# Three gate projections in the scans, 9,800 columns per scan step, preparation two gaps apart, and another order of scores and transposes in the attention

## The chip, the core and the metric

The kernel runs on one core of one Trainium2 chip. The core has five engines, each with its own instruction stream: TensorE (PE, matrix products; its weight loads, PEld, overlap them), VectorE (DVE), ScalarE (ACT), GpSimd (POOL) and SyncE (SP, which issues the DMAs of this kernel). Each of them executes its stream in order, and waits on semaphores for the others. The metric is the device time of one execution in microseconds (us); less is better. Every time given for a program is a median over several executions, and one further execution is recorded by the hardware profiler.

## The reference

One layer of a hybrid backbone: a gated DeltaNet of 8 heads and a grouped-query attention of 8 query heads read the same normalised input through one projection `w_in`; each head's output is multiplied by silu of a gate that is also a projection of that input; `w_out` closes the layer.

```python
def mixer(h, hc, w_in, conv_w, a_log, dt_bias, gdn_norm_w, q_norm_w, k_norm_w, w_out, cos, sin, with_ctx):
    qkv_g, z_g, gates, q_a, k_a, v_a, z_a = split_proj(h @ w_in)
    qkv_gc, z_gc, gates_c, q_ac, k_ac, v_ac, z_ac = split_proj(hc @ w_in)
    ql, kl, vl, bl, gl = gdn_inputs(qkv_g, gates, conv_w, a_log, dt_bias)
    qc, kc, vc, bc, gc = gdn_inputs(qkv_gc, gates_c, conv_w, a_log, dt_bias)
    ...
    o_lf, _ = chunk_gated_delta(ql, kl, vl, gl[0], bl[0], s_cf)
    ...
    gdn_lat = (rms_norm(o_gdn, gdn_norm_w).reshape(B, L, GDN_WIDTH) * jax.nn.silu(z_g))
    qa, ka, va = attn_heads(q_a, k_a, v_a, q_norm_w, k_norm_w)
    qa, ka = apply_rope(qa, cos, sin), apply_rope(ka, cos, sin)
    ...
    attn_lat = block_attention(qa, k_all, v_all) * jax.nn.silu(z_a)
    y = jnp.concatenate([gdn_lat, attn_lat], axis=-1) @ w_out
```

There are 512 latent tokens, 256 context tokens, a model width of 2048 and a head width of 128, all in float32. `z_g` and `z_a` are the gates: 8 heads of 128 columns each.

## The kernel before

Every matrix product of the projections is made of three, of a high and a low part of each operand (`whi`, `wlo`: ACT copies the high part of a weight piece, POOL subtracts to get the low one, both of 128x512). A projection of one head for the latent tokens is 16 blocks of rows x 3 = 48 matmuls of 512 columns; with the context tokens it has 48 of 256 columns more.

PE's order is the order in which the program is written (`manual_schedule` for PE), from the first scan to the end of the attention. DVE, ACT, POOL and SP are ordered by a scheduler in the first part, with raised priority for the recurrence; in the attention DVE, ACT and POOL stand in the written order as well. The stages, by the profile's time, are:

- *The start* (to 242 us): modulation, the projections of head 0, decay gates, preparation of head 0.
- *The scans* (242 to 922 us): `gdn_scan(h)` for 8 heads, one after the other. A head has 12 steps. A step is a recurrence between PE, DVE and ACT: `ks` (keys and queries on the state), `rh` on DVE, `ts` (solved block), `vs` and `vn` on ACT, the state's update `ts`, `st` on DVE, `o`. The generator yields up to three times in a step, with F1, F2, F3 = 3400, 2200, 2800; at each yield the loop *pulls* so many columns of other projections from `feeding()` (one matmul of 512 columns, or of 512 and 256, at a time). A yield is a gap, or slot; a head has 35 of them. Between heads the loop pulls on until the next head's k, q and v are made ("forced" pulls).
- *Preparation*: `gdn_prep(h + 1)` is a generator too, and its groups run in the slots of `PREP_AT` of head h: transposes of the keys t1, t2, t3 with their squares on ACT (`NT`, `ss`), Gram matrices `gq`, `gc`, the solve of small blocks (`NE` on DVE, through DRAM: `nd`, `NE`, `nd2`, `DD`), transposes of the values, then `DT` (a transpose of DD on DVE) and the products pxa, pxb, pxy in slots 27 to 33. t1 and t3 have one PSUM bank in turn, t2 and gq another. The end of a scan, its *tail* (squares, norm, scaling of `oq`, transposes `ot`), runs under the next head's slots.
- *Feeding*: q, k, v of head 1; three of the attention's keys and values (`kva`); k, q, v of the heads 2 to 7; the last `kva`; the eight attention queries `qa`, which go through DRAM (`qad`).
- *The attention* (922 to 1225 us): 17 units u, of which each has the scores of one head's half (`attn_scores`, softmax on DVE and ACT) and the transposes and values of the unit before (`attn_pt`, `attn_values`). `fill(n)` puts n times three matmuls of the gate projections between them: `fillers()` makes all 16 gates (64 pieces of 12 matmuls), and drives `gate_rows()`, which sums the rows of the residual's gate on ACT and POOL (`graw`, `gacc`). FS, FP, FQ, FR = 3, 3, 1, 3 are the numbers of fills behind the scores, behind each of three transposes, behind the values and at the unit's end. `z_over` turns a finished gate into silu and multiplies it with `M`, which holds the 16 heads' outputs.
- *The output projection* (from 1225 us).

In columns, the pulls ask for 110,500 ahead of the first scan, and for 12 x 8,400 - 3,400 = 97,400 in each scan. What there is to pull is 7 x 48 x 2048 (k, q, v) + 4 x 48 x 768 (kva) + 8 x 48 x 512 (qa) = 1,032,192.

## Time and profile before

| | |
|---|---|
| median of 3 runs | 1426.57 us (1420.46 to 1427.27) |
| the profiled execution | 1422.1 us |
| its span, first to last instruction | 1420.3 us |
| granted TensorE clock, mean | 0.982 |
| DMA | 161.95 MB, mean 114 GB/s |

In the rows of the profile that follow below, a line is "engine line operation output<-inputs"; buffer numbers are left out of the names, so `tsh` is the `ts` tile of any head and step, `rh` the `r` tile, `sth` the state. A row of waits has who waited for whom, the total in us, the number of waits and the longest. A row of the timeline begins with start and duration in us, and has the idle time ahead of it, with what ended it, in square brackets. Matmuls are pipelined: what one costs is the distance to the start of the next, not its duration.

### The profile page before, as it was taken

The numbers are of one execution on the slowest core, as the hardware profiler recorded it, in microseconds if no ns is written. First come the engines' busy times: TensorE is split into PE (matmuls) and PEld (weight loads), VectorE is DVE, ScalarE is ACT, GpSimd is POOL, SyncE is SP. The second block draws the span as 40 slices with busy tenths as digits, with TensorE's granted clock in tenths as the row PEclk, the third lists the DMA queues.
The fourth block names the chain that finished last, engine by engine and source line by source line (L and its number), as shares of the span: only waits on it lengthen the run. The fifth ranks groups of instructions, "written<-read, shape, count | busy, mean of one in ns | idle before, by whom it ended". The sixth has DMA issues, their size and how long they took to land. (4 is left out here: it accounts for less than half of the span.)

```text
span 1420.3 us, 24982 instructions
## 1 busy us (share of the span) xinstructions
PE 1282.4 (90%) x9406; PEld 1024.6 (72%) x9406; DVE 741.2 (52%) x1642; ACT 608.5 (43%) x1511; POOL 533.0 (38%) x477
## 2 busy tenths in 40 slices
PE   3888888999998989899898988989999999999997
PEld 1455677888777777777777767777777777777785
DVE  3444694533666766576756343155555555644322
ACT  4111343343545455544545444355555554433221
POOL 1011212334344343434343444466666665112320
PEclk9999999999999999999999999999999999999999
DMA  9999622322222213132222343454444442474202
GB/s 310 277 279 283 162 66 58 73 73 74 61 54 64 55 46 73 50 62 58 54 65 57 84 135 86 132 179 119 127 134 121 117 125 76 165 235 148 89 31 103
DMA packets 263323, 161.95 MB, mean 114 GB/s; under 512 B 62946, under 2 KB 236091, under 8 KB 262179
## 3 DMA queue, kind: packets, MB, share of 16 engines
q1 hardware_dynamic: 263203, 160.36, 41.0%
q8 instruction: 74, 1.21, 0.4%
q14 instruction: 46, 0.38, 0.1%
HBM read 147.54 MB, written 12.77 MB: 113 GB/s over the span
## 5 line engine op out<-in xcount | busy, mean ns | idle before, releaser
L122 POOL TENSOR_TENSOR wlo_z<-wraw_z,whi_z 128x512 fp32r<-128x512 f32 x64 | 92.5, 1448 | 80.4 <-ACT whi_z L121 72.1
L214 POOL TENSOR_TENSOR sdh<-sth,egl 128x256 f32<-128x256 f32 x80 | 55.7, 696 | 143.3 <-DVE sth L756 69.6
L1186 PE MATMUL zl<-hhL,whi_z 128*128 128x512 f32 x256 | 107.4, 420 | 0.0
L1186 PE MATMUL zl<-hlL,whi_z 128*128 128x512 f32 x256 | 101.6, 397 | 0.0
L1186 PE MATMUL zl<-hhL,wlo_z 128*128 128x512 f32 x256 | 101.3, 396 | 0.2 <-POOL wlo_z L122 0.2
L735 ACT ACTIVATE oqh<-ksh,egsw 64x128 f32<-64x128 f32 x128 | 46.6, 364 | 118.8 <-DVE rh L730 118.0
L730 DVE SCALAR_TENSOR_TENSOR rh<-ksh,negeg,vtokh 64x128 f32<-64x128 f32 x176 | 61.3, 348 | 53.7 <-PE ksh L718 41.5
L1225 POOL TENSOR_TENSOR gacc<-graw,gacc 128x512 f32<-128x512 f32 x60 | 85.1, 1418 | 0.5
L139 PE MATMUL po<-wlo_wo,mh 128*128 128x512 f32 x192 | 76.9, 401 | 1.8 <-DVE wlo_wo L122 1.8
L138 PE MATMUL po<-whi_wo,mh 128*128 128x512 f32 x192 | 77.0, 401 | 1.6 <-DVE M L214 1.1
L140 PE MATMUL po<-whi_wo,ml 128*128 128x512 f32 x192 | 76.7, 400 | 0.0
L756 DVE TENSOR_TENSOR sth<-sdh,tsh 128x256 f32<-128x256 f32 x80 | 33.7, 421 | 77.6 <-PE tsh L750 56.3
L122 DVE TENSOR_TENSOR wlo_wo<-wraw_wo,whi_wo 128x512 fp32r<-128x512 f32 x48 | 37.8, 794 | 59.5 <-ACT whi_wo L121 59.3
L1321 POOL TENSOR_TENSOR yx<-yx,tt 128x512 f32<-128x512 f32 x12 | 17.2, 1446 | 127.8 <-DVE tt L214 127.8
L750 PE MATMUL tsh<-vsh,ktok 128*128 128x128 f32 x352 | 59.2, 292 | 5.7 <-ACT vnh L746 5.7
L122 POOL TENSOR_TENSOR wlo_qa<-wraw_qa,whi_qa 128x512 fp32r<-128x512 f32 x32 | 41.4, 1295 | 53.0 <-ACT whi_qa L121 44.1
L743 ACT ACTIVATE vsh<-tsh,cch 128x128 f32<-128x128 f32 x88 | 32.3, 368 | 66.9 <-PE tsh L739 64.2
L750 PEld LDWEIGHTS tsh<-vsh,ktok 128*128 128x128 f32 x352 | 47.8, 195 | 18.0 <-ACT vnh L746 14.5
L815 DVE TENSOR_TENSOR ptl<-pt,pth 128x512 fp32r<-128x512 f32 x48 | 32.8, 683 | 53.5 <-ACT pth L814 53.5
L1103 DVE TENSOR_REDUCE mx<-s 128x1 f32<-128x768 f32 x32 | 30.5, 953 | 53.9 <-PE s L140 53.9
L1186 PEld LDWEIGHTS zl<-hhL,wlo_z 128*128 128x128 f32 x256 | 48.3, 189 | 12.4 <-POOL wlo_z L122 0.6
L1186 PEld LDWEIGHTS zl<-hhL,whi_z 128*128 128x128 f32 x256 | 48.5, 189 | 11.4 <-ACT whi_z L121 2.5
(398 smaller groups left out, 4045.7 us busy)
## 6 DMA issues: line engine op xcount, KB each, us to landing
wada<-in_w_ada SPq DMA_DIRECT2D x128, 256.0 KB, 5.2
wraw_z<-in_w_in SPq DMA_DIRECT2D x64, 256.0 KB, 2.9
graw<-in_w_ada SPq DMA_DIRECT2D x64, 256.0 KB, 3.0
wraw_wo<-in_w_out SPq DMA_DIRECT2D x48, 256.0 KB, 2.9
wraw_qa<-in_w_in SPq DMA_DIRECT2D x32, 256.0 KB, 2.8
wraw_q<-in_w_in SPq DMA_DIRECT2D x28, 256.0 KB, 2.9
wraw_k<-in_w_in SPq DMA_DIRECT2D x28, 256.0 KB, 2.9
wraw_v<-in_w_in SPq DMA_DIRECT2D x28, 256.0 KB, 2.9
```

Source lines behind the costliest of these rows:

```text
L122: (lo_eng or G).tensor_tensor(out=lo, in0=raw, in1=hi, op=ALU.subtract)
L138: T.matmul(out, lhsT=lh, rhs=rh, start=start, stop=False, skip_group_check=True)
L139: T.matmul(out, lhsT=lh, rhs=rl, start=False, stop=False, skip_group_check=True)
L140: T.matmul(out, lhsT=ll, rhs=rh, start=False, stop=stop, skip_group_check=True)
L214: eng.tensor_tensor(out=out, in0=x, in1=y, op=ALU.mult)
L730: V.scalar_tensor_tensor(out=r[rows], in0=ks[rows, d], scalar=gsc["negeg"][rows, gcol:gcol + 1], in1=vtok[rows, p], op0=ALU.mult, op1=ALU.add)
L735: S.activation(oq[rows, v, p - 2], ks[rows, d], AF.Copy, scale=gsc["egsw"][rows, gcol:gcol + 1])
L750: T.matmul(ts[:, d], lhsT=ktok[:, p, half], rhs=vs, start=True, stop=True, skip_group_check=True)
L756: V.tensor_tensor(out=sn, in0=sd, in1=ts[:, 0:2], op=ALU.add)
L815: V.tensor_tensor(out=lo, in0=ps_ap, in1=hi, op=ALU.subtract)
L1186: T.matmul(pl, lhsT=lw, rhs=rt[:, k], start=st, stop=sp, skip_group_check=True)
L1225: G.tensor_tensor(out=acc, in0=raw, in1=acc, op=ALU.add)
```

## The change

Four things are changed. (1) F1, F2, F3 become 3900, 2700, 3200: 9,800 columns per step, 113,700 per scan. The gates of three attention heads (`feed_za`, 3 x 48 x 512 columns) are added to the end of the feeding and go through DRAM (`zad`); there are then 1,105,920 columns to pull. `fillers()` leaves these three out, and units 0 to 2 of the attention take them from `M` (`zae`, `silu`); `attn_values` multiplies by half. (2) The groups of the preparation stand in slots 0, 2, 4, 6, 8, 10, 12 instead of 0, 1, 2, 3, 5, 7, 9; the last four stay. (3) The feeding puts one `kva` behind head 1 and each of the heads 2 and 3, and one `qa` behind each of the heads 4 to 7. (4) In a unit of the attention the first two transposes come ahead of the scores; FS, FV, FQ, FR = 4, 4, 1, 3 fills stand behind the scores, ahead of the values, behind them and at the end; the steps of the query's normalisation follow the scores. The rows of the residual's gate advance twice in four fills from the sixth piece on, instead of nine times in 32 fills from the start.

```diff
--- before.py
+++ after.py
@@ -17,8 +17,9 @@
 D = 2048
 KT = D // 128
 CA_BUFS = 1
-FS, FP, FQ, FR = 3, 3, 1, 3
+FS, FV, FQ, FR = 4, 4, 1, 3
 GB = 3
+NZA = 3
 SEQ = 512
 CTX = 256
 NTOK = SEQ + CTX
@@ -887,8 +888,8 @@
         A["qt"] = [apr.tile([128, SEQ], F32R, tag=i, bufs=2, name=f"{i}0") for i in ("qTh", "qTl")]
         split_from(tp.rearrange("p t c -> p (t c)"), *A["qt"])
 
-    F1, F2, F3 = 3400, 2200, 2800
-    PREP_AT = (0, 1, 2, 3, 5, 7, 9, 27, 29, 31, 33)
+    F1, F2, F3 = 3900, 2700, 3200
+    PREP_AT = (0, 2, 4, 6, 8, 10, 12, 27, 29, 31, 33)
 
     def first_of_all():
         return tc.high_priority(offset=2500)
@@ -912,6 +913,7 @@
         G.memset(IBs[i], 0.0)
     kvd = dram.tile([4, 128, NTOK], F32, name="kvd")
     qad = dram.tile([NH, 128, SEQ], F32, name="qad")
+    zad = dram.tile([NZA, 128, SEQ], F32, name="zad")
     fed = set()
 
     def feed_k(h):
@@ -942,28 +944,37 @@
         SY.dma_start(kvd[i, :, 0:CTX], tmp[:, 2:2 + CTX])
         SY.dma_start(kvd[i, :, CTX:NTOK], tmp[:, CTX + 4:NTOK + 4])
 
-    def feed_qa(h):
-        pl = PP.tile([128, SEQ], F32, tag="pl", name=f"qal{h}")
-        yield from proj_steps(COL_QA + h * 128, f"qa{h}", pl)
+    def feed_out(col, nm, dst):
+
+        pl = PP.tile([128, SEQ], F32, tag="pl", name=f"{nm[0]}al{nm[1:]}")
+        yield from proj_steps(col, nm, pl)
         tmp = next_craw()
         S.copy(tmp[:, CTX + 4:NTOK + 4], pl)
-        SY.dma_start(qad[h], tmp[:, CTX + 4:NTOK + 4])
+        SY.dma_start(dst, tmp[:, CTX + 4:NTOK + 4])
+
+    def feed_qa(h):
+        yield from feed_out(COL_QA + h * 128, f"q{h}a", qad[h])
+
+    def feed_za(h):
+        yield from feed_out(COL_ZA + h * 128, f"z{h}a", zad[h])
 
     def feeding():
 
         yield from feed_q(1)
         yield from feed_k(1)
         yield from feed_v(1)
-        for i in range(3):
-            yield from feed_kva(i)
+        yield from feed_kva(0)
         for h in range(2, NH):
             yield from feed_k(h)
             yield from feed_q(h)
             yield from feed_v(h)
+            yield from feed_kva(h - 1) if h < 4 else feed_qa(h - 4)
         yield from feed_kva(3)
         fed.add("kva")
-        for h in range(NH):
+        for h in range(4, NH):
             yield from feed_qa(h)
+        for h in range(NZA):
+            yield from feed_za(h)
 
     feed = feeding()
     debt = [0]
@@ -1134,7 +1145,7 @@
             mm3(op, vah[:, j, vsl], val[:, j, vsl], pts[j // 2][0][:, j % 2], pts[j // 2][1][:, j % 2], j == 0, j == 5)
         m = M[8 + h][:, qp * 256:qp * 256 + 256]
         if (h, qp) in early:
-            mul(V, m, m, op)
+            V.scalar_tensor_tensor(out=m, in0=m, scalar=0.5, in1=op, op0=ALU.mult, op1=ALU.mult)
         else:
             S.copy(m, op)
         done.add((h, qp))
@@ -1154,11 +1165,13 @@
             if (i - 8, qp) in done:
                 V.scalar_tensor_tensor(out=m, in0=e2, scalar=0.5, in1=m, op0=ALU.mult, op1=ALU.mult)
             else:
-                V.tensor_scalar(out=m, in0=e2, scalar1=0.5, scalar2=None, op0=ALU.mult)
+                S.copy(m, e2)
                 early.add((i - 8, qp))
 
+    zs = list(range(8)) + list(range(8 + NZA, 16))
+
     def z_piece(n):
-        i, kq = divmod(n, 4)
+        i, kq = zs[n // 4], n % 4
         col = (COL_ZG if i < 8 else COL_ZA - 1024) + i * 128
         src = w_in[kq * 512:(kq + 1) * 512, col:col + 128].rearrange("(k p) c -> p k c", p=128)
         return wpiece(src, f"z{i}_{kq}", 128)
@@ -1168,12 +1181,10 @@
         pieces = [z_piece(0), z_piece(1)]
         over = None
         yield
-        for n in range(64):
-            i, kq = divmod(n, 4)
-            if n + 2 < 64:
+        for n in range(4 * len(zs)):
+            i, kq = zs[n // 4], n % 4
+            if n + 2 < 4 * len(zs):
                 pieces.append(z_piece(n + 2))
-            for _ in range(1 + (n % 8 == 7)):
-                next(rows, None)
             if kq == 2 and outs:
                 gate_out(*outs.pop(0))
             hi, lo = pieces.pop(0)
@@ -1184,6 +1195,8 @@
                 for lw, rt, st, sp in ((hi[:, k4], hhL, k == 0, False), (hi[:, k4], hlL, False, False),
                                        (lo[:, k4], hhL, False, k == KT - 1)):
                     T.matmul(pl, lhsT=lw, rhs=rt[:, k], start=st, stop=sp, skip_group_check=True)
+                if n >= 6 and k4 % 2 == 0:
+                    next(rows, None)
                 if over is not None and k == 1:
                     z_over(*over)
                 yield
@@ -1233,6 +1246,8 @@
     qcs = {i: attn_q(i) for i in (1, 2)}
     for i in range(8):
         SY.dma_start(M[i], o_d[i])
+    for i in range(NZA):
+        SY.dma_start(M[8 + i], zad[i])
     rows = gate_rows()
     next(rows)
     gen = fillers()
@@ -1251,23 +1266,31 @@
     for u in range(2 * NH + 1):
         h, qp = divmod(u, 2)
         more = h + 1 < NH
-        prs = None
+        prs, pts = None, []
+        if before is not None:
+            pts = [attn_pt(*before, j2) for j2 in range(2)]
         if h < NH:
             prs = attn_scores(h, qp, *qt)
-            fill(FS + 8 * (before is None))
-        pts = []
-        for j2 in range(3):
-            if before is not None:
-                pts.append(attn_pt(*before, j2))
-            if prs is not None and j2 < 2:
-                attn_over(*prs[j2])
-            if qp == 1 and more and j2 in (0, 2):
+            if qp == 1 and more:
+                next(qns)
+            fill(FS + 5 * (before is None))
+        if before is not None:
+            pts.append(attn_pt(*before, 2))
+        if prs is not None:
+            attn_over(*prs[0])
+            if qp == 1 and more:
                 qn = next(qns)
-            if before is not None:
-                fill(FP)
+            attn_over(*prs[1])
         if before is not None:
+            fill(FV)
             attn_values(before[0], before[1], pts)
-            fill(FQ)
+        if u < NZA:
+
+            e = ap_.tile([128, SEQ], F32, tag="ze", bufs=2, name=f"zae{u}")
+            S.activation(e, M[8 + u], AF.Tanh, scale=0.5)
+            silu(V, M[8 + u], M[8 + u], e)
+            early.update(((u, 0), (u, 1)))
+        fill(FQ)
         if more:
             if qp == 0:
                 qns = attn_norm(h + 1, qcs.pop(h + 1))
@@ -1276,7 +1299,7 @@
                     qcs[h + 3] = attn_q(h + 3)
             else:
                 qt = attn_qt(h + 1, qn)
-            fill(FR)
+        fill(FR)
         before = h, qp, prs
     for _ in gen:
         pass
```

The scheduler moves instructions as follows. ACT, at the start of the scan of head 3, where the preparation of head 4 begins. Names have the head's number (`oth2`: head 2; `t1h4`: head 4). Before:

```order
L743 ACTIVATE vsh3_0_5408<-tsh3_0_5406,cch3_4582 128x128
L769 ACTIVATE och2_5360,msh2_5359<-oqh2_4503 128x128
L194 ACTIVATE cacc_v4_5378<-craw0_1460,cvT_80 128x770
L769 ACTIVATE och2_5360,msh2_5359<-oqh2_4503 128x128
L509 COPY ktok0_1555<-t1h4_5419 64x4x128
L769 ACTIVATE och2_5360,msh2_5359<-oqh2_4503 128x128
L511 ACTIVATE NTh4_5418,ssh4_5417<-t1h4_5419 128x128
L554 ACTIVATE grh4_5414<-grh4_5414 128x768
L773 ACTIVATE oqh2_4503<-oqh2_4503,msh2_5359 128x128 x4
L511 ACTIVATE NTh4_5418,ssh4_5417<-t1h4_5419 128x128
L515 COPY ktok0_1555<-t2h4_5420 64x4x128
```

And with the change:

```order
L774 ACTIVATE oqh2_4378<-oqh2_4378,msh2_5296 128x128 x4
L122 CAST whi_q0a_1_5448<-wraw_q0a_1_5446 128x512
L122 CAST whi_q0a_2_5479<-wraw_q0a_2_5477 128x512
L184 COPY craw0_1460<-vx4_5170 128x256
L187 COPY craw0_1460<-vl4_5169 128x512
L744 ACTIVATE vsh3_0_5407<-tsh3_0_5405,cch3_4491 128x128
L195 ACTIVATE cacc_v4_5379<-craw0_1460,cvT_80 128x770
L510 COPY ktok0_1555<-t1h4_5419 64x4x128
L512 ACTIVATE NTh4_5418,ssh4_5417<-t1h4_5419 128x128 x4
```

The scaling of head 2's output by its norm (L773, now L774) stood among the squares of t1 (L511), and now stands ahead of the scan's first step; the four squares follow each other.

DVE, in steps 6 to 8 of the same scan, where the solve ends (`NEh4`, `tmh4`) and the transpose of its result (`DTh4<-DDh4`) follows. Before:

```order
L608 TENSOR_TENSOR NEh4_5561<-NEh4_5561,tmh4_5573 96x14
L198 SCALAR_TENSOR_TENSOR cacc_k5_5745<-craw1_1461,cvT_80,cacc_k5_5745 128x256 x2
L211 SCALAR_TENSOR_TENSOR kc5_5742<-craw1_1461,cacc_k5_5745 128x2x64
L756 TENSOR_TENSOR sth3_6_5848<-sdh3_6_5817,tsh3_6_5836 128x256
L211 SCALAR_TENSOR_TENSOR kc5_5742<-craw1_1461,cacc_k5_5745 128x2x64
L730 SCALAR_TENSOR_TENSOR rh3_7_5863<-ksh3_5405,negeg_87,vtokh3_4703 64x128 x2
L756 TENSOR_TENSOR sth3_7_5891<-sdh3_7_5866,tsh3_7_5878 128x256
L198 SCALAR_TENSOR_TENSOR cacc_q5_5895<-craw0_1460,cvT_80,cacc_q5_5895 128x512 x2
L730 SCALAR_TENSOR_TENSOR rh3_8_5920<-ksh3_5405,negeg_87,vtokh3_4703 64x128 x2
L631 STREAM_TRANSPOSE DTh4_5680<-DDh4_5679 128x384
```

And with the change:

```order
L609 TENSOR_TENSOR NEh4_5623<-NEh4_5623,tmh4_5635 96x14
L757 TENSOR_TENSOR sth3_6_5882<-sdh3_6_5824,tsh3_6_5840 128x256
...
L731 SCALAR_TENSOR_TENSOR rh3_7_5891<-ksh3_5404,negeg_87,vtokh3_4646 64x128 x2
...
L757 TENSOR_TENSOR sth3_7_5927<-sdh3_7_5894,tsh3_7_5913 128x256
L199 SCALAR_TENSOR_TENSOR cacc_k5_5856<-craw0_1460,cvT_80,cacc_k5_5856 128x256
L212 SCALAR_TENSOR_TENSOR kq5_5852<-craw0_1460,cacc_k5_5856 128x4x64 x2
L212 SCALAR_TENSOR_TENSOR kc5_5853<-craw0_1460,cacc_k5_5856 128x2x64
L632 STREAM_TRANSPOSE DTh4_5744<-DDh4_5743 128x384
L731 SCALAR_TENSOR_TENSOR rh3_8_5942<-ksh3_5404,negeg_87,vtokh3_4646 64x128 x2
```

The solve's end has moved to just ahead of `sth3_6`, and the transpose from behind `rh3_8` to ahead of it.

PE, at the end of the last scan, where the transposes of the last head (`oth7`) and then the first scores (`s0_0`) stand. Before:

```order
L156 MATMUL qal6_9577<-hhL_70,whi_qa6_3_9660 128x512
L156 MATMUL qal6_9577<-hlL_71,whi_qa6_3_9660 128x512
L777 MATMUL oth7_9672<-cmain_77,oqh7_8949 128x128 x4
L156 MATMUL qal6_9577<-hhL_70,wlo_qa6_3_9661 128x512
L156 MATMUL qal6_9577<-hhL_70,whi_qa6_3_9660 128x512
```

And with the change, where no projection is left behind them:

```order
L157 MATMUL zal2a_9858<-hhL_70,whi_z2a_3_9947 128x512
L157 MATMUL zal2a_9858<-hlL_71,whi_z2a_3_9947 128x512
L157 MATMUL zal2a_9858<-hhL_70,wlo_z2a_3_9948 128x512
L778 MATMUL oth7_9979<-cmain_77,oqh7_9228 128x128 x4
L139 MATMUL s0_0_10061<-kTh_9258,qTh0_9876 128x512
L140 MATMUL s0_0_10061<-kTl_9259,qTh0_9876 128x512
```

Before, 28 matmuls of the attention's queries lay between the last `oh7` and `oth7` and 52 more between `oth7` and the scores; now 18 of the third gate lie ahead of it, and none behind.

## The prediction

> **What bounds the kernel now.** I read the busy times first, then stage by stage, because an average over 1420 us hides which engine ends last where. The stages are the scans, the attention and the output projection.
>
> ```profile
> PE 1282.4 (90%) x9406; PEld 1024.6 (72%) x9406; DVE 741.2 (52%) x1642; ACT 608.5 (43%) x1511; POOL 533.0 (38%) x477
> ...
> 241.65:921.85 680.20, 625.09 (x5524) 522.01 (x5525) 373.89 (x933) 312.87 (x889) 272.81 (x264) 0.98 0.28 70
> 921.85:1225.29 303.44, 286.70 (x1505) 233.98 (x1504) 161.29 (x251) 163.37 (x347) 188.05 (x136) 0.99 0.43 122
> ```
>
> In the stretches (length, then busy PE, PEld, DVE, ACT, POOL, clock, DMA share, GB/s), PE is busy 92% and 94%. Apart from its own weight loads, which overlap it, nothing is over 62%; DMA is at 28% and 43%. PE's order is written by hand, so its time is its work plus the places where the next instruction isn't ready. Moving matmuls on PE gains nothing by itself; a gain can only come from idle time. So the waits of PE are the view that counts:
>
> ```profile
> PE tsh L739 <- DVE rh L730: 16.6, 22, 3.0
> PE t3h L521 <- ACT NTh L511: 16.4, 5, 3.3
> PE tsh L750 <- ACT vnh L746: 5.7, 10, 0.9
> PE ksh L716 <- DVE sth L756: 4.9, 10, 0.6
> PE qtp L819 <- DVE ktok L811: 3.3, 1, 3.3
> PE gqh L561 <- ACT NTh L517: 3.0, 6, 0.8
> PE kx L158 <- ACT craw L183: 2.2, 5, 0.4
> PE ksh L721 <- DVE sth L756: 1.5, 2, 1.2
> ...
> PE qtp L819 <- DVE qn L1083: 10.3, 7, 3.0
> PE o L139 <- DVE ptl L815: 5.6, 16, 0.6
> ```
>
> These are total us, times, longest; the first eight rows are of the scans, the last two of the attention. The long ones are dearer than they look. Here is PE's clock in single windows (length, PE busy, clock):
>
> ```profile
> 441.04:444.45 3.41, 2.73 (x10) 0.50 0.00 0
> 444.45:447.86 3.41, 2.84 (x28) 1.00 0.29 79
> ...
> 755.07:761.89 6.82, 6.06 (x31) 0.50 0.16 38
> ...
> 953.04:956.45 3.41, 2.72 (x9) 0.50 0.54 157
> ...
> 441.72 0.69 PE L521 MATMUL t3h<-cmain,kc 128*128 128x128 f32 x2 [3.27 <-ACT NTh L511]
> ...
> 438.36 1.28 ACT L773 ACTIVATE oqh<-oqh,msh 128x128 f32<-128x128 f32 x4 [1.59 <-POOL msh L208]
> 439.54 0.26 ACT L511 ACTIVATE NTh<-t1h 128x128 f32<-128x128 f32 x1
> ```
>
> At the end of the 3.27 us wait for t3 the clock stands at 0.50 for one window of 3.41 us; half the work of it is lost, 1.7 us. The five t3 waits lie between 441 and 755 us and each has such a window behind it, the last one two, so a wait costs 5 us and not 3.3. The last rows show why PE waits: on ACT, the previous head's scaling (L773) waits for POOL, and the squares of t1 that must free the bank stand behind it.
>
> **The change part by part.** The price of the moved work:
>
> ```profile
> 909.95 0.40 PE L156 MATMUL qal<-hhL,whi_qa 128*128 128x512 f32 x1
> ...
> 915.55 0.40 PE L156 MATMUL qal<-hhL,whi_qa 128*128 128x512 f32 x1
> ```
>
> There are 24 steps between these two rows, so 0.233 us for 512 columns. *Three gate projections* are 3x48 = 144 such matmuls, 33.6 us, out of the attention and into the scans: zero on PE. Their 12 splits, 3 copies, 3 stores and 3 loads lie beside PE's work (ACT 46%, POOL 40%, DMA 28% busy there).
>
> *Fill per step.* A step asks for 9,800 columns where it asked for 8,400. Each gap gets 400 to 500 columns, 0.18 to 0.23 us, and where PE waited there it waits that much less. The rows of tsh and ksh (16.6, 5.7, 4.9, 1.5) are 44 waits: 44 x 0.2 = 9 us, and with gaps too short for that view I take **10** (bounds 5 and 17). Is there enough to fill with? Before, the pulls are 110,500 ahead of the scans and 8 x 97,400 in them, and the 1,032,192 columns leave 142,000 to run bare. After: 8 x 113,700 + 110,500 of 1,105,920, with forced pulls between scans of 9,000 to 22,000 columns. The supply lasts to the end of the last scan, with about 5,900 columns left.
>
> *Groups two gaps apart.* t3 now comes four gaps after t1 instead of two: 13,000 columns (5.9 us) against 6,200 (2.8 us), which is about the 3.3 us that it waited. And the order on ACT has the scaling L774 ahead of the copies of v, so it no longer stands among the squares. t3's waits go (**16.4**), their six half-clock windows go (6 x 1.7 = **10.2**), and of gq's 3.0 I take **2.5**. What is late next is the end of the preparation, whose last groups stay at 27 to 33:
>
> ```profile
> L608 DVE TENSOR_TENSOR NEh<-NEh,tmh x14: 164/196/1205, 461.4 to 475.6; 96x14 f32<-96x14 f32 x2, 96x26 f32<-96x26 f32 x2, 96x36 f32<-96x36 f32 x2, 96x44 f32<-96x44 f32 x2
> ...
> L626 SPq DMA_DIRECT2D DDh<-nd x4: 303/462/468, 479.9 to 481.3; - x4
> ...
> DMA to landing us min/median/max: 3.6/3.6/3.6
> ...
> 472.15 0.42 DVE L756 TENSOR_TENSOR sth<-sdh,tsh 128x256 f32<-128x256 f32 x1
> ...
> 489.12 0.42 DVE L756 TENSOR_TENSOR sth<-sdh,tsh 128x256 f32<-128x256 f32 x1 [0.36 <-ACT whi_v L121]
> ```
>
> From the solve's last row (475.6) to DD's landing (481.3 + 3.6, an estimate from the landing of the other DMA) are about 9 us. In the new order the solve ends just ahead of sth_6, and the transpose that needs DD stands behind sth_7 and some convolution rows and ahead of rh_8. The two sth rows are three steps apart, 5.7 us each; with the added columns a step is some 6 us. One step and 1.5 us for those rows make 7.5 against 9: DVE can be held for up to 1.5 us, of which PE's gaps cover a part. I take 0.5 us for each of 7 heads, **-4**; bounds 0 and -14 (2 us each).
>
> *Order of feeding.* kva and qa now stand between v(h) and k(h+1). k's first context matmul, which waited for v's copy (kx 2.2), is spared in four heads: **2**.
>
> *End of the scans.* Only 18 matmuls (4.2 us) now lie between the last oh and the transposes of the last head, where 28 lay:
>
> ```profile
> 902.43 0.49 PE L759 MATMUL oh<-vnh,IB 128*128 128x128 f32 x2
> ...
> 909.28 0.38 PE L777 MATMUL oth<-cmain,oqh 128*128 128x128 f32 x2
> ```
>
> The chain through DVE, ACT and POOL took up to 6.5 us, so PE waits 2.3 us. Whether that costs a half-clock window, the trace answers with the shortest wait that did:
>
> ```profile
> 842.96 0.46 PE L739 MATMUL tsh<-rh,UU 128*128 128x128 f32 x2 [1.83 <-DVE rh L730]
> ...
> 843.81:847.22 3.41, 3.41 (x14) 0.50 0.51 107
> ```
>
> So 1.83 us can be enough, and I take 2.3 + 1.7 = **-4**. The Trainium skill ("TensorE: Matmul & The Clock Gate", Part 1) says that the clock falls after an idle window of about 3.4 us; by that the 1.7 here would be nothing. The trace agrees for t3's waits and not for this row, so the row decides.
>
> *Start of the attention.* ACT's tanh of M8 (zae0) stands ahead of the copy qn1, and M8 is the ninth of eleven loads on SP:
>
> ```profile
> L1235 SPq DMA_DIRECT2D M<-o_d x8: 424/432/1390, 923.1 to 927.4; - x8
> ...
> DMA to landing us min/median/max: 5.6/5.6/5.6
> ```
>
> With SP's issues at 0.43 us it lands some 13 us behind the last head's transposes, and qn1 follows at 14.4. PE comes to the bank that qn1 frees after 2.1 us (4,608 columns of scores), ten fills of three matmuls (7.0), three more (2.1) and some 1.3 of transposes, 12.5 us: **-2**, bounds 0 and -7.
>
> *Order within the attention.* A unit fills 12 times 3 matmuls, where it filled 16 times. The normalisation's multiplies come right behind the scores, eight fills ahead of the q transposes, where they came one fill and the values ahead. Of 10.3 I keep 4 (RoPE's product waits behind POOL's queue): **6.3**, and the half-clock window at 953.04: **1.7**. The values come four fills behind the last transpose of the scores; of 5.6, **4** goes.
>
> Sum: 10 + 16.4 + 10.2 + 2.5 + 2 + 6.3 + 1.7 + 4 = 53 gained, 4 + 4 + 2 = 10 given back: 43. The profiled execution took 1422.1 us (span 1420.3), and 1422 - 43 = 1379. The median shown is 1426.57, 4.5 above that execution; I say **1380**.
>
> **The rivals.** *POOL becomes the bound of the attention.* The gate rows now run at two for four fills, six per unit:
>
> ```profile
> L122 POOL TENSOR_TENSOR wlo_z<-wraw_z,whi_z 128x512 fp32r<-128x512 f32 x62 | 89.9, 1453 | 77.4 <-ACT whi_z L121 69.1 <-DMA M<-o_d 7.8 <-DMA wraw_z<-in_w_in 0.2
> L1225 POOL TENSOR_TENSOR gacc<-graw,gacc 128x512 f32<-128x512 f32 x60 | 85.1, 1418 | 0.5
> L214 POOL TENSOR_TENSOR rt<-qn,tabq 128x512 f32<-128x512 f32 x7 | 9.2, 1311 | 7.7 <-DVE qn L214 7.7
> L208 POOL TENSOR_TENSOR hss<-hss,expo 128x4 f32<-128x4 f32 x7 | 7.1, 1014 | 19.0 <-DVE hss L1073 15.3 <-DMA qc<-qad 3.6
> ...
> L122 POOL TENSOR_TENSOR wlo_z<-wraw_z,whi_z x64: 1287/1302/1762, 917.0 to 1212.3; 128x512 fp32r<-128x512 f32 x64
> ```
>
> A unit has 3 x 1.45 + 6 x 1.42 = 12.9 us of these two, and 16.3 / 16 = 1.0 of RoPE and norm: 13.9. PE has 12 fills (8.4), scores and values (2.1 each) and its transposes, some 14.5. At the longest split (1.76 for each of the nine) POOL has 16.8. If it runs 1.5 us over PE in each of ten units, 1395. Against it: the rows stop after eleven units, and the weights are split two pieces ahead. The Trainium skill ("GPSIMD Engine Reference", 1. Specifications) has GpSimd share its SBUF interfaces with VectorE, in contention when that reads two SBUF operands; the spread from 1.29 to 1.76 us agrees.
>
> *The fill hides nothing.* If the waits in the gaps are chains that only shift (DVE's convolutions moved into them), the 10 fall away and t3 keeps half of its 26.6: 1403.
>
> *The groups don't part.* If ACT's squares are late by something else than the two gaps and L773, t3 still waits with its windows: 27 us more, 1407.
>
> *Slower than before.* DVE takes its instructions in order. If DD lands late (SP has a weight load ahead of it that waits for a buffer), the transpose blocks rh_8 and the whole recurrence. The price is the delay over the 0.5 us, for 7 heads. It cancels the gain from about 6 us per head on; 8 us, with a half-clock window of 1.7 at each, make 1379 + 7 x 9.2 = 1443. For it: the weight load stands there in the order. Against it: before, the transpose started after 0.3 us of idle, with no wait for a DMA.
>
> **How the numbers follow.** Forecast 0.70 (1380; own range 1362 to 1396 from the bounds of the terms), POOL 0.12 (1395), no hiding 0.07 (1403), groups 0.06 (1407), slower 0.05 (1443). The range holds the first three cases: 1360 to 1404. A measurement of this kernel tells a difference from no change above about 0.5%, 7 us; the first four cases are faster by more, but I leave 0.03 for a mix of costs that ends within it: faster 0.92, same 0.03, slower 0.05.
>
> **What would show it.** Right: no waits of t3h for NTh, fewer windows at 0.50 in the scans, about 75 us between starts of heads where forced pulls are left out, attention near 260 us. Wrong: PE waiting for rh with DTh's transpose just ahead of it on DVE; zl waiting for wlo_z in the attention; qtp still waiting for qn; a long wait at the last head's transposes.

## The result, and the profile after

| | before | after |
|---|---|---|
| median, same chip | 1425.35 us, 7 runs (1420.46 to 1427.27) | 1409.70 us, 7 runs (1404.02 to 1413.92) |
| ratio of the times | | 0.9897, 95% interval 0.9872 to 0.9922 |
| the profiled execution, its span | 1422.1, 1420.3 us | 1413.92, 1412.1 us |

The kernel is 16 us faster, where 43 were forecast; the time lies above the range. The profiled execution is the slowest of the seven. First the span by stages, with the time that PE's clock stood at half in each. The stages are cut at the first `tsh` of the scans, the first score and the first product of the output.

| us | start | scans | attention | output |
|---|---|---|---|---|
| before | 241.7 | 680.2 | 303.4 | 195.0 |
| forecast for after | 241.7 | 680.7 | 259.8 | 195.0 |
| after | 248.4 | 682.8 | 283.9 | 197.1 |
| at half clock, before | 6.8 | 30.7 | 3.4 | 9.9 |
| at half clock, after | 27.3 | 6.8 | 27.3 | 7.8 |

The forecast's terms give the scans 33.6 more for the moved gates, 41.1 saved and 8 given back, and the attention 33.6 and 12 less and 2 back. The scans came within 2.1 us of that. The attention missed by 24.1 us; this is the error. A stage in one profiled execution has a spread of its own: among the kernels of this document, six that have the same code in the scans took 682.0 to 686.8 us there, and five with this attention 278.4 to 283.9. So the miss is 19 to 24 us, and a difference of 5 us in a stage says little. Here are both stages of after in the view of stretches (length, busy PE, PEld, DVE, ACT, POOL, clock, DMA share, GB/s):

```profile
248.37:931.16 682.79, 644.95 (x5668) 541.72 (x5669) 376.56 (x933) 319.38 (x903) 287.62 (x276) 1.00 0.30 74
931.16:1215.06 283.90, 261.02 (x1362) 214.44 (x1362) 164.41 (x251) 154.68 (x327) 170.76 (x124) 0.95 0.44 126
```

The clock has changed places: the scans rose from 0.98 to 1.00, the attention fell from 0.99 to 0.95. The waits of PE in the scans of after:

```profile
PE tsh L740 <- DVE rh L731: 14.7, 17, 2.1
PE ksh L722 <- DVE sth L755: 5.1, 4, 2.3
PE ksh L717 <- DVE sth L757: 4.2, 11, 0.5
...
PE tsh L751 <- ACT vsh L744: 3.2, 4, 0.8
...
PE kx L159 <- ACT craw L942: 2.7, 3, 1.2
PE tsh L740 <- DVE UU L686: 0.9, 1, 0.9
PE oth L778 <- ACT oqh L774: 0.6, 1, 0.6
```

There is no wait for t3 any more (16.4 before) and none for gq (3.0). The waits of tsh and ksh, which the fill was to shorten, held 28.7 us before, in the four rows that the prediction adds up. The like ones hold 28.0 now: 14.7, 5.1, 4.2 and 3.2 above, and two of 0.4 that are not shown (the wait for UU is not one of them). And in the attention:

```profile
PE qtp L820 <- DVE mx L1124: 14.2, 6, 2.7
PE pt L1133 <- ACT qn L1081: 3.2, 1, 3.2
PE o L139 <- ACT pth L815: 2.3, 3, 1.5
PE o L140 <- DVE ptl L816: 1.4, 4, 0.3
```

The q transposes wait longer than before, 14.2 us against 10.3, in six heads; the values wait less, 3.7 against 5.6. The releaser's name (`mx`, the reciprocal that stands next on DVE) is only the neighbour of what PE waits for, the sum of RoPE. DVE's timeline in one unit of after shows it:

```profile
986.86 1.01 DVE L215 TENSOR_TENSOR qn<-qn,hss 128x512 f32<-128x512 f32 x1
990.96 0.69 DVE L816 TENSOR_TENSOR ptl<-pt,pth 128x512 fp32r<-128x512 f32 x1 [3.10 <-ACT pth L815]
991.57 0.15 DVE L1124 RECIPROCAL mx<-mx 128x1 f32<-128x1 f32 x1
991.76 0.65 DVE L1125 TENSOR_SCALAR pr<-pr,mx 128x768 f32<-128x768 f32 x1
992.33 1.79 DVE L215 TENSOR_TENSOR qn<-qn,tabq 128x512 f32<-128x512 f32 x1
994.16 1.66 DVE L1094 TENSOR_TENSOR qn<-qn,rt 128x512 f32<-128x512 f32 x1
```

The last two rows are the second step of the normalisation. DVE stands idle for 3.10 us ahead of them, because the low part of the third transpose (`ptl`), which waits for ACT, stands first in its order. ACT's timeline shows why its high part (`pth`) is late:

```profile
986.85 0.90 ACT L1119 ACTIVATE pr<-s,mx 128x768 f32<-128x768 f32 x1 [2.85 <-DVE mx L1114]
...
988.61 0.72 ACT L1236 ACTIVATE graw<-graw,scol 128x512 f32<-128x512 f32 x1
989.23 0.61 ACT L122 CAST whi_z<-wraw_z 128x512 fp32r<-128x512 f32 x1
989.74 0.73 ACT L1236 ACTIVATE graw<-graw,scol 128x512 f32<-128x512 f32 x1
990.36 0.57 ACT L815 CAST pth<-pt 128x512 fp32r<-128x512 f32 x1
```

PE's part of this transpose was done by about 986.3. But the two exps of the softmax stand ahead of it on ACT, and they start only at 986.85, after 2.85 us of waiting for the maxima of the scores on DVE; two gate rows and a weight split follow. PE's q transpose then starts at 995.97 after 2.70 us of idle, and this is what the clock does (PE alone: length, busy, clock):

```profile
991.34:994.75 3.41, 1.59 (x9) 1.00 0.60 159
994.75:1001.58 6.83, 5.61 (x18) 0.50 0.60 169
```

Four of the six waits have such windows at half clock behind or in them, three of them 6.83 us long, 23.9 us together. (One of the long ones, from 1028.89, opens before its q transpose waits, behind a wait of 1.49 us for the values.) PE is busy for 19.6 us of these 23.9, so 9.8 us of work are lost.

### The profile page after: what moved, and what is told of

Its sections match the earlier page's. It is cut to its first block, busy times and chain, and to the rows that moved or that the text cites. A ratio compares the mean times of both kernels' runs of the same rounds, so it can differ in the third digit from the quotient of the medians.

```text
span 1412.1 us, 24988 instructions
## 1 busy us (share of the span) xinstructions
PE 1282.5 (91%) x9406; PEld 1031.0 (73%) x9406; DVE 747.5 (53%) x1643; ACT 608.3 (43%) x1509; POOL 529.4 (37%) x477
## 4 chain that ended last, share of the span: by engine, by line
PE 55%; DVE 17%; DMA 8%; issue 8%; ACT 7%; POOL 4%; SPq 2%; POOLq 0%; ACTq 0%; DVEq 0%
PE zl L1197 6%; PE vl L157 5%; DMA wada<-in_w_ada 4%; PE kl L157 3%; PE vx L159 3%; DVE cacc_k L199 2%; DVE cacc_v L199 2%; PE kvl L157 2%; PE po L140 2%; PE tsh L751 2%; PE po L141 2%; PE po L139 2%; PE ql L157 2%; PE kx L159 2%; PE tsh L740 2%
## 5 line engine op out<-in xcount | busy, mean ns | idle before, releaser
L1238 POOL TENSOR_TENSOR gacc<-graw,gacc 128x512 f32<-128x512 f32 x60 | 89.3, 1488 | 43.3 <-ACT graw L1236 30.0
L1197 PE MATMUL zl<-hhL,whi_z 128*128 128x512 f32 x208 | 88.0, 423 | 0.0
L123 POOL TENSOR_TENSOR wlo_z<-wraw_z,whi_z 128x512 fp32r<-128x512 f32 x52 | 70.5, 1358 | 45.0 <-ACT whi_z L122 43.8
L1197 PE MATMUL zl<-hlL,whi_z 128*128 128x512 f32 x208 | 84.9, 408 | 0.0
L1197 PE MATMUL zl<-hhL,wlo_z 128*128 128x512 f32 x208 | 84.8, 408 | 0.1
L199 DVE SCALAR_TENSOR_TENSOR cacc_v<-craw,cvT,cacc_v 128x512 f32<-128x512 f32 (+1 forms) x64 | 44.0, 734 | 38.8 <-ACT cacc_v L195 38.5
L751 PE MATMUL tsh<-vsh,ktok 128*128 128x128 f32 x352 | 55.6, 281 | 3.6 <-ACT vsh L744 3.2
L323 POOL TENSOR_TENSOR wlo<-wraw,whi 128x384 fp32r<-128x384 f32 x16 | 16.0, 1006 | 110.4 <-ACT whi L322 110.4
L122 ACT CAST whi_wo<-wraw_wo 128x512 fp32r<-128x512 f32 x48 | 29.3, 618 | 61.4 <-PE po L141 37.7
L751 PEld LDWEIGHTS tsh<-vsh,ktok 128*128 128x128 f32 x352 | 47.8, 192 | 10.1 <-ACT vsh L744 4.6
L255 PE MATMUL ada<-wada,cs 128*32 128x256 f32 x512 | 42.3, 417 | 13.9 <-DMA wada<-in_w_ada 13.8
```

The source lines that it names most:

```text
L123: (lo_eng or G).tensor_tensor(out=lo, in0=raw, in1=hi, op=ALU.subtract)
L199: V.scalar_tensor_tensor(out=x, in0=raw[:, i0 + j:i0 + j + m], scalar=w(j), in1=x, op0=ALU.mult, op1=ALU.add)
L751: T.matmul(ts[:, d], lhsT=ktok[:, p, half], rhs=vs, start=True, stop=True, skip_group_check=True)
L1197: T.matmul(pl, lhsT=lw, rhs=rt[:, k], start=st, stop=sp, skip_group_check=True)
L1238: G.tensor_tensor(out=acc, in0=raw, in1=acc, op=ALU.add)
```

## The experiments

**The attention: who holds the q transposes?** Theory A: the place of the second step on DVE. Theory B: the residual's gate rows, now two for four fills, load ACT and POOL. The first experiment moves one line: the second step now stands ahead of the third transpose, and so also of two short operations of the softmax (0.8 us in the timeline above). The second experiment restores the pacing of the rows.

```diff
+        if prs is not None and qp == 1 and more:
+            qn = next(qns)
         if before is not None:
             pts.append(attn_pt(*before, 2))
         if prs is not None:
             attn_over(*prs[0])
-            if qp == 1 and more:
-                qn = next(qns)
```

> The changed kernel with one line moved: the second step of the query's normalisation (two products and a sum on DVE) is issued ahead of the third transpose of the scores, where the change has it behind. Theory A (DVE's order): in the changed kernel that step stands on DVE behind the third low part (ptl), which waits on ACT for its high part behind two exps and the gate rows; so the sum ends 3 us after PE came to the q transposes. Then the waits of PE for the q transposes fall from 14.2 us (6 times) to under 4, the windows at half clock in the attention from 5 (27 us long) to at most 2, the attention stage from 284 us to 260 to 268, and the whole by 16 to 26 us against the changed kernel, to about 1388. Theory B (ACT and POOL are too full with the gate rows, whatever the order): the wait only changes its place, to the values (o) or stays at the transposes with over 10 us in all; the stage stays over 277.

Measured: 1393.52 us (4 runs), ratio 0.9798 [0.9768, 0.9829]. The attention takes 267.3 us, 16.6 less than with the change and 11 less than the shortest of the five. The waits of PE there, and DVE in the same unit:

```profile
PE o L140 <- DVE ptl L816: 5.6, 9, 1.0
PE o L139 <- ACT pth L815: 4.5, 5, 1.6
PE pt L1133 <- ACT qn L1081: 2.5, 1, 2.5
```

```profile
978.10 1.05 DVE L215 TENSOR_TENSOR qn<-qn,hss 128x512 f32<-128x512 f32 x1
980.57 0.69 DVE L215 TENSOR_TENSOR qn<-qn,tabq 128x512 f32<-128x512 f32 x1 [1.43 <-POOL rt L215]
981.30 1.65 DVE L1094 TENSOR_TENSOR qn<-qn,rt 128x512 f32<-128x512 f32 x1
982.87 0.68 DVE L816 TENSOR_TENSOR ptl<-pt,pth 128x512 fp32r<-128x512 f32 x1
```

The second step now lies in the time that DVE spent idle, and ptl follows without a gap. No q transpose waits; 3.4 us are left at half clock, where 27.3 stood. That is as A expected. Part of the gain is given back: the values wait 10.1 us, where they waited 3.7. The other side's experiment has nine rows in 32 fills, 3.4 in a unit instead of 6:

```diff
+            for _ in range(1 + (n % 8 == 7)):
+                next(rows, None)
...
-                if n >= 6 and k4 % 2 == 0:
-                    next(rows, None)
```

> The changed kernel with the gate rows paced as before the change: nine rows in 32 fills, from the first piece on and ahead of a piece's matmuls, where the change has two rows in four fills from the sixth piece on. Theory A (DVE's order): ACT has 1.5 rows fewer per unit, some 1 us less between the exps and the third high part; the wait at the q transposes falls from about 2.7 us to 1.5 to 2.2 each and most windows at half clock may go, the whole is 5 to 15 us faster than the changed kernel. Theory B (load of the rows): the wait goes to under 0.5 us each and the whole gains 20 us or more, to under 1390.

Measured: 1414.04 us (5 runs), 0.9936 [0.9911, 0.9962]. The largest sum of waits in its attention is still this:

```profile
PE qtp L820 <- DVE mx L1124: 15.7, 7, 3.1
```

With fewer rows on ACT and POOL the q transposes wait no less: B falls, and with it the part of A's expectation that gave this run a gain. The time of the whole says less here. The attention takes 278.9 us, as in the shortest of the five; but the slower pacing leaves 6 of the 64 rows for the output, which takes 207.3 us where it took 197.1. That POOL isn't the bound its own waits in after say too (who waits for whom, total, times, longest):

```profile
POOL wlo_z L123 <- ACT whi_z L122: 42.8, 12, 8.6
POOL gacc L1238 <- ACT graw L1236: 30.0, 10, 7.5
```

The next one puts the units' old order back (all three transposes behind the scores, the steps of the normalisation behind the first and the third), with 12 fills a unit.

```diff
-        prs, pts = None, []
-        if before is not None:
-            pts = [attn_pt(*before, j2) for j2 in range(2)]
+        prs = None
...
+            fill(2 + 8 * (before is None))
+        pts = []
+        for j2 in range(3):
+            if before is not None:
+                pts.append(attn_pt(*before, j2))
+            if prs is not None and j2 < 2:
+                attn_over(*prs[j2])
+            if qp == 1 and more and j2 in (0, 2):
...
+            if before is not None:
+                fill(2)
```

> The changed kernel with the order within a unit of the attention as before the change (scores first, a transpose and two fills three times, then the values), and the same 12 fills per unit. It tells what the new order alone is worth. Theory A: in the old order the sum of the normalisation also stood late, with 1.5 us of wait in each of 7 heads and 16 fills; with 12 it waits 2 to 3 us in each, and each such wait has a window at half clock. The stage then takes as long as in the changed kernel, 278 to 290 us, and the whole is within 8 us of it. If the new order was the harm, this kernel is 15 us or more faster; if it was worth what the prediction said, it is 10 us or more slower.

Measured: 1414.89 us (4 runs), 0.9938 [0.9913, 0.9962]; the attention takes 287.6 us, 3.7 more than with the change, with 6.8 us at half clock. Now the transposes and values wait (12.8 and 9.9 us, for ptl), and the q transposes less (6.7). By itself, then, the new order was worth 4 to 9 us beside the five attentions that have it, where 12 were forecast: it exchanged waits. The one line in it is worth 11 to 17, beside the same five.

Is the same line worth as much in the kernel before? There the second step stands behind the third ptl too.

```diff
-            if qp == 1 and more and j2 in (0, 2):
+            if qp == 1 and more and j2 in (0, 1):
```

> The kernel before with one edit: the second step of the normalisation behind the second transpose instead of the third. Theory A (the multiplies of the normalisation wait on DVE behind the third ptl): the seven q transposes no longer wait (10.3 us and one half-clock window of 1.7), the attention 7 to 12 us shorter, 1413 to 1419. Rival: the wait of the kernel before has another cause (RoPE's product on POOL is late behind the gate rows and splits): the seven waits of about 1.5 us stay, and the time is within 3 us of the kernel before.

Measured: 1448.16 us (6 runs), 1.0166 [1.0139, 1.0192]. Slower, and both expectations missed. The q transposes don't wait any more, as A says; but PE waits in the values, in the view of waits and on DVE:

```profile
PE o L139 <- DVE ptl L815: 30.0, 17, 5.6
```

```profile
987.20 0.68 DVE L815 TENSOR_TENSOR ptl<-pt,pth 128x512 fp32r<-128x512 f32 x1
...
988.75 1.75 DVE L214 TENSOR_TENSOR qn<-qn,tabq 128x512 f32<-128x512 f32 x1
990.53 1.63 DVE L1083 TENSOR_TENSOR qn<-qn,rt 128x512 f32<-128x512 f32 x1
992.09 0.68 DVE L815 TENSOR_TENSOR ptl<-pt,pth 128x512 fp32r<-128x512 f32 x1
```

Here DVE has no idle time to give: it works without a gap from 982.82 to 992.77, so the 3.4 us of the step push the third ptl back by as much, and the values, which come ahead of the q transposes, wait 3.92 us in this head. The attention is 24.0 us longer than before, with 34.1 us of it at half clock. So in both kernels the order on DVE decides which of PE's instructions waits, and the move gained where the step found idle time, as in the first experiment, and lost where it found none.

Two attempts to better the first one: the early gates' silu behind the q transposes, and then the third transpose right behind the scores as well.

```diff
-        if u < NZA:
-            e = ap_.tile([128, SEQ], F32, tag="ze", bufs=2, name=f"zae{u}")
-            S.activation(e, M[8 + u], AF.Tanh, scale=0.5)
...
             else:
                 qt = attn_qt(h + 1, qn)
+        if u < NZA:
+            e = ap_.tile([128, SEQ], F32, tag="ze", bufs=2, name=f"zae{u}")
+            S.activation(e, M[8 + u], AF.Tanh, scale=0.5)
...
         fill(FR)
```

> The first experiment's kernel (normalisation ahead of the third transpose) with the silu of the three early gates issued behind the query's transposes of its unit, where the change has it ahead of them. If ACT was held by the load of M8 in the first unit, PE's one wait for qn (2.5 us, with a window at half clock) goes, and the whole is 2 to 6 us faster than that kernel; if M8 lands late for other reasons, the wait moves to the next transposes and the whole is within 2 us of it.

Measured: 1396.56 us (5 runs), 0.9804 [0.9784, 0.9824]: no gain over the first experiment. The wait for qn is gone, as it should be if the load of M8 held ACT; in its place pt's waits for ptl grew from 1.0 to 3.8 us.

```diff
         if h < NH:
             prs = attn_scores(h, qp, *qt)
+        if before is not None:
+            pts.append(attn_pt(*before, 2))
+        if h < NH:
             if qp == 1 and more:
                 next(qns)
             fill(FS + 5 * (before is None))
-        if before is not None:
-            pts.append(attn_pt(*before, 2))
```

> The kernel before this one, and the third transpose of the scores issued right behind the scores, ahead of the fills: its high part then stands on ACT ahead of the two exps and of the gate rows, its low part on DVE ahead of the normalisation. If the values wait (10 us in 14 times) because ACT comes late to that high part, these waits fall to under 3 us and the attention is 6 to 9 us shorter; against it, the reductions on DVE start 0.7 us later and PE may wait for the bank of the first transpose, up to 1 us in each of 15 units, by which the whole would be up to 8 us slower.

Measured: 1417.51 us (10 runs), 0.9950 [0.9934, 0.9967]. Expected faster, and slower by 21 us than without it: the waits of pt for ptl (16.0, 8 times, longest 5.8) and of the q transposes (10.1) come back. The move doesn't do what was expected of it. The exps are issued together with the scores, so ACT still has them ahead of the third high part: in one unit of this run they start at 1020.37 and 1021.26, and the high part at 1022.14. And PE now comes to the third transpose too early. The transposes have two banks in turn, and the first one's is free only when DVE has made its low part; that waited 3.36 us for ACT and starts at 1017.07, and PE's transpose starts at 1017.82 after 3.04 us of idle.

**The scans: which part freed t3, and what does the fill hide?** Three parts are taken back one at a time, then two together, the gates staying in the scans.

```diff
-    PREP_AT = (0, 2, 4, 6, 8, 10, 12, 27, 29, 31, 33)
+    PREP_AT = (0, 1, 2, 3, 5, 7, 9, 27, 29, 31, 33)
```

> The changed kernel with the preparation's groups in the old slots 0, 1, 2, 3, 5, 7, 9. Theory S (the two gaps are what freed t3): t3 waits again for the squares, 2.5 to 3.5 us in five heads, with windows at half clock, and the scans are 20 to 27 us longer. Theory L (the scaling of the previous head on ACT, which no longer stands among the squares, was the cause): t3 waits under 1 us in each head without windows, and the scans are within 8 us of the changed kernel's 683 us.

Measured: 1414.57 us (4 runs), 0.9936 [0.9916, 0.9957]. No wait for t3 comes back, as theory L expected, and the scans are 6.1 us longer, little more than the spread of equal scans.

```diff
-        yield from feed_kva(0)
+        for i in range(3):
+            yield from feed_kva(i)
...
-            yield from feed_kva(h - 1) if h < 4 else feed_qa(h - 4)
...
-        for h in range(4, NH):
+        for h in range(NH):
```

> The changed kernel with the feeding in the old order (three kva behind head 1, then k, q, v of each head, all qa at the end and the three gates behind them); the groups stay two gaps apart. In the scheduler's order the scaling of the previous head then stands among the squares of t1 again. Theory L (the place of the scaling is what made t3 wait, and the feeding order moved it): t3 waits again, by 0.5 to 3 us in four or five heads, because the spacing gives at most 3.1 us more; the scans are 5 to 20 us longer than 683 us. Theory S (the spacing is enough by itself): t3 waits under 0.3 us in every head.

Measured: 1434.20 us (4 runs), 1.0067 [1.0044, 1.0089]. The scaling stands among the squares of t1 again, and t3 doesn't wait either, as theory S expected. But the scans are 24.6 us longer. They have 27.3 us at half clock where 6.8 stood, and PE waits for UU (6.6 us, with the change 0.9), for grh (4.4, once) and for the issue of pxb (3.3, once). How the order of feeding brings these about was not followed up. With both taken back:

> The changed kernel with the old feeding order and the old places of the preparation, (0, 1, 2, 3, 5, 7, 9, ...); the new F and the three gates in the scans stay. It is the fourth corner of the square of feeding and places. Theory S (the wait for t3 needs both the scaling among the squares of t1 and the two-gap distance to t3; either one alone removes it): PE waits for t3 come back, five or so of about 3 us with a half-clock window behind each, scans 10 to 25 us over the run with the old feeding alone (707.4), so about 1445 to 1460. Theory F (the t3 waits are gone because the longer gaps give time, whatever the order): no t3 waits, scans within 6 us of 707.4.

Measured: 1438.12 us (4 runs), 1.0110 [1.0084, 1.0136]. Up to 840 us PE waits as follows, among others:

```profile
PE t3h L522 <- ACT NTh L512: 5.9, 4, 2.2
...
PE gqh L562 <- ACT NTh L518: 4.4, 5, 1.0
```

Both are back, t3 at a third of its former size, and the scans are 8.8 us longer than with the old feeding alone, a little under what theory S expected, and with no more time at half clock (27.3 us in both). So, with the longer fill, either part alone frees t3: two gaps more, or the scaling out of the way. That the longer fill, which this run keeps, took the other two thirds is likely, but no run tests it by itself. Then the fill:

```diff
-    F1, F2, F3 = 3900, 2700, 3200
+    F1, F2, F3 = 3400, 2200, 2800
```

> The changed kernel with 3400, 2200, 2800 columns per gap as before (8,400 per step), all else of the change kept. What the gaps don't take is then made bare between the heads and at the end of the scans. Theory G (the gaps hid what the prediction said): the scans' waits for rh, sth and the like grow by 8 to 15 us, and the scans take 692 to 700 us where the changed kernel has 683. Theory N (the gaps hide nothing, the waits only shift): the scans stay within 4 us of 683.

Measured: 1424.48 us (10 runs, 1414.30 to 1429.92), 0.9990 [0.9965, 1.0015]; the scans of the profiled execution, the fastest of the ten, are 12.5 us longer, as theory G expected. The waits for rh, sth and the like grow by only 3 of these (31.1 us against 28.0); another 7.6 are new waits for the issue of pxb. And last, on the version of the first experiment, the gates taken back into the attention:

```diff
-FS, FV, FQ, FR = 4, 4, 1, 3
+FS, FV, FQ, FR = 5, 5, 2, 4
...
-NZA = 3
+NZA = 0
```

> The version with the second step of the normalisation ahead of the third transpose, and with the three gates left in the attention: all 16 are made by its fills (5 behind the scores, 5 ahead of the values, 2 and 4). The last scan then lacks some 68,000 of its 113,700 columns. Theory M (moved matmuls cost the same in either place, zero on PE, as the prediction had it): scans 34 us shorter, attention 34 longer, time within 5 us of 1393.5. Theory N (the gates fill gaps of the last scan that would stand open): in 7 or so of its 12 steps PE waits for the recurrence, 2 to 3 us each with half-clock windows; attention 34 longer, scans only 10 to 25 shorter, 1403 to 1418.

Measured: 1433.34 us (6 runs), 1.0065 [1.0048, 1.0082]: 40 us over the first experiment, and both theories missed. The scans are only 8.8 us shorter, and the last scan, which now runs out of columns, has waits in place of the gates (total, times, longest, from 838 to 916 us):

```profile
PE tsh L740 <- DVE rh L731: 6.9, 7, 2.2
PE qtp L820 <- DVE ktok L812: 4.7, 1, 4.7
PE oth L778 <- ACT oqh L774: 4.3, 1, 4.3
PE tsh L751 <- ACT vnh L747: 3.6, 5, 0.9
```

In the view of stretches, the last but two of the numbers is the clock:

```profile
838.00:916.00 78.00, 54.38 (x265) 43.16 (x263) 31.73 (x74) 33.11 (x111) 26.81 (x28) 0.80 0.28 87
```

It is 0.80 on average in the last scan. The attention is 54.4 longer: 33.6 for the gates, and the rest in waits and windows that the added fills bring (o for ptl 14.0 us, where 5.6 stood, and zl for its weights 7.4, where none stood).

To add the scans up, I take from the one trace of each kernel the time from the first `tsh` of one head to that of the next, less its projections at the 0.233 us for 512 columns of the prediction:

| us | heads 0 to 6 | of it projections | rest | last head to scores | rest |
|---|---|---|---|---|---|
| before | 579.5 | 357.7 | 221.9 | 100.7 | 38.9 |
| feeding and places old | 620.4 | 400.1 | 220.3 | 95.9 | 43.0 |
| feeding old | 611.8 | 400.1 | 211.7 | 95.7 | 42.8 |
| places old | 601.4 | 398.7 | 202.7 | 87.6 | 33.3 |
| fill old | 599.7 | 391.2 | 208.5 | 95.7 | 33.9 |
| after | 594.2 | 398.7 | 195.6 | 88.6 | 34.3 |
| gates left in the attention | 595.4 | 398.7 | 196.7 | 77.8 | 57.1 |

The rests of after are 30.9 us under those of before. The longer fill by itself (second row against first) gives nothing; the places take 8.6 off it, the feeding 17.6 in seven heads and 9.7 in the last; taken from the whole, the fill is worth 12.9. The parts don't add up one by one.

## Why the prediction was wrong

**The step that failed** is the order within the attention: "The normalisation's multiplies come right behind the scores, eight fills ahead of the q transposes ... Of 10.3 I keep 4 (RoPE's product waits behind POOL's queue)", with 6.3 us for it and 1.7 for the window. Only the first multiply came right behind the scores. The sum that the transposes need stands in the second step, behind the third ptl, and that one waits for ACT. Counted in fills, the second step gained one: five and the values lie between it and the q transposes, where four and the values lay (three behind the third transpose and one behind the values; the prediction has one). I looked for the hold-up on POOL, whose product was ready at 989.25 in the unit above, 3 us before DVE began the step. I did not follow DVE's order between the two places, where the step's two operations queue behind an instruction that isn't theirs. In place of 4 us the waits are 14.2, and 9.8 us of work are lost at half clock beside them, where nothing was forecast. That is 20 us of the 24. The first experiment takes both away with one line, and gives 6.4 back in the waits of the values; in the run with the old pacing, with fewer rows on ACT and POOL, the waits stay.

Of the other terms of the attention, the start was given 2 us and cost 3.2 with a window behind it that loses 1.4 (4.6 together), and the values gained 1.9 instead of 4. These two bring the sum to 24.7, where the miss is 24.1. The rival that POOL becomes the bound didn't come about.

**The scans** came out right in the sum, less so in the terms. t3's and gq's waits went, as forecast, and the work lost at half clock (half of PE's busy time there) fell from 13.7 to 3.2 us, 10.5 where 10.2 stood. The reason holds in a weaker form: the spacing or the order of ACT is enough. The 10 of the gap fill can't be found where they were put: the waits for rh and st are as long as before. The fill is needed all the same, as its own experiment shows, where PE waits 20.7 us for rh and 7.6 for the issue of pxb; with the old feeding and places it gained nothing. Why it counts only together with them was not settled. The 8 us to be given back did not come: DVE's transpose of DD held nothing, and at the end the wait is 0.6, not 2.3. The 2 of the kx term did not come either (2.2 before; 2.7 after, for another copy). "Zero on PE" for the moved gates was too cautious: they fill the last scan's gaps, and cost it 9.9 us (from 77.8 to the 87.7 of the first experiment's kernel) and not 33.6. On the other side, without the gates, and with the last scan short of columns, the scans take 673.2 us, only 7.0 under the kernel before, where the other terms promised 33. These errors cancel: that the sum came out so close is luck.

The trace also has 6.7 us more in the start, whose code the change doesn't touch, and 2.1 more in the output: 24.1 + 6.7 + 2.1 + 2.1 is the distance from the forecast to this span.

The rival that ends slower was a late DD, and there is no sign of it. The version of the first experiment is faster than both kernels: its ratio to the kernel before is 0.9798, the change's 0.9897, and the intervals lie apart.

## What to carry to other kernels

When an instruction is moved nearer to its input on one engine, follow its consumer's chain through every in-order engine it passes, and ask what stands ahead of each link there: an instruction of another chain that waits holds all behind it. Move a chain's link into a stretch in which its engine stands idle; where the engine works without a gap, the same move only hands the wait to the neighbour. And parts of a change that share one supply (here the columns that fill the gaps) can't be priced one by one: take the whole apart on the chip.

## What the runs showed of the hardware

The half-clock windows follow a rule that I had not expected. They lie on a grid of 3.41 us that runs on by itself, and what decides is how long PE was busy in the window before. In the thirteen traces, of the windows at full clock that lie wholly between 245 and 1210 us, all 81 in which PE was busy for under 1.4 us were followed by one at half clock, 22 of the 36 between 1.4 and 1.7, and 1 of the 3,421 above. The way back takes more: of the windows at half clock, all 20 with PE busy for under 2.7 us were followed by another, 3 of the 6 at 2.70 to 2.74, and none of the 101 above. This is why some are double: from 994.75 on, PE was busy for 2.19 of the first 3.41 us.

So the place of a wait on the grid counts as much as its length. In after, the wait of 2.70 us that ends at 995.97 left, with a short one before it, 1.59 us in the window before 994.75, and the clock fell; here a wait of 2.69 us, ended at 1068.22, is cut by the grid:

```profile
1063.02:1066.43 3.41, 1.94 (x9) 1.00 0.58 186
1066.43:1069.84 3.41, 1.62 (x9) 1.00 0.67 194
1069.84:1073.25 3.41, 3.41 (x23) 1.00 0.45 129
```

Neither window is left under 1.4 us, and the clock stays. By these counts a wait in an otherwise busy stretch does nothing up to some 1.7 us (3.41 - 1.7), one of 2.7 does it or not, and one of over 4.0, twice 3.41 - 1.4, does it wherever it lies. The Trainium skill ("TensorE: Matmul & The Clock Gate", Part 1) has a free-running window of the same length, with which the traces agree; it has the clock fall after an idle window, and here one that is a little under half busy is enough. The windows ahead of t3's in the kernel before, where the prediction saw agreement, were not idle throughout either: PE was busy in them for 0.14 to 0.87 us.

Code that none of these kernels changes varies too. The start took 239.6 to 248.4 us in the profiled executions; it had 6.8 us at half clock in the kernel before (241.7) and 27.3 in the change (248.4), but also 20.5 in the run with the old pacing, which took 241.7. The ten runs with the old fill spread over 15.6 us. In the five traces with this attention the q transposes wait for 13.4 to 15.1 us, but 13.7 to 27.3 us stand at half clock. That the grid, whose place against the program may differ from one execution to the next, makes this spread is a guess that no run tested.
